# A hybrid decoder step in split fp16: first pairs by seven products at later blocks, spread forms of x, and range checks by ScalarE

## The chip, the cores and the metric

The kernel is one program on one core of a Trainium2 chip. Its time is the device time of one execution in microseconds (us). A core has TensorE (PE) for matrix products, VectorE (DVE), ScalarE (ACT) and GpSimd (POOL), and SyncE (SP), which here only issues transfers. PE's loads of stationary weights are listed apart as PEld; they run beside the matmuls. The DMA engines are shared by the queues of SP (q1), GpSimd (q0) and ScalarE (q10).

## The reference

One layer for 256 prompt tokens and 8 sample tokens, together T = 264 columns, with D_MODEL = 2048 and D_FF = 5504:

```python
h = h + 0.5 * swiglu(rmsnorm(h, norm_ffn1), ffn1_gate, ffn1_up, ffn1_down)
mix, C, n, m, buf = mixing_block(rmsnorm(h, norm_mix), w_in, ..., w_out, C_in, n_in, m_in, conv_in)
h = h + mix
h = h + 0.5 * swiglu(rmsnorm(h, norm_ffn2), ffn2_gate, ffn2_up, ffn2_down)
y = rmsnorm(h, norm_final)

def swiglu(x, wg, wu, wd):
    return (jax.nn.silu(x @ wg) * (x @ wu)) @ wd
```

The mixing block holds four mLSTM heads and a short gated convolution. All weights and inputs are float32. The change lies in the two SwiGLU stages, called the first and the second FFN here.

## The kernel before, in words

**Arithmetic.** Activations lie channels by tokens. Each float32 operand is scaled and split into an fp16 high part and an fp16 low part, and a product of 128 x 128 weights with 264 columns is three matmuls (`three`, L285 to L288): high weight by high x, high weight by low x, low weight by high x. `high` (L216) makes the high part on ScalarE, L219; `low` (L223) makes the low part on VectorE, L227. A weight tile is 128 x 8 x 128 in float32 (`wraw`), which becomes `whi` and `wlo`. `fetch` (L233) issues the load of the next tile of the plan on SP, and then its high and low parts. There are six buffers of each (`AHEAD` = 5, and one), and fetches run up to five tiles ahead of the products. With `lag` set, a tile's low part is issued one fetch later.

**Plan and start.** `weight_plan` (L82) lists the weight loads in order. The first four products of the first FFN (gate and up of blocks 0 and 1) run together in `products4` (L487), k by k, since x and the weights arrive k by k: `FIRST` (L45) lists the units as (first k, number of k, first product, number of products). A unit's weights are loaded and split while the one before is multiplied, and `ahead` (L854) loads h and cuts x from it.

**FFN.** D_FF is 43 blocks of 128, in two halves of 22 and 21 blocks (`HALVES`). A plain block is a gate product and an up product of 16 k each, one PSUM bank each (`product`, L290), followed by the scaling with the norm (L825, L831), Silu on ScalarE (L828) and the product of both (`activated`, L732). After each half come the products with the down weights.

**By seven products.** For the blocks of the list `SEVEN`, gate and up, the two halves of k and the two halves of the tokens are the 2 x 2 x 2 blocks of a product that needs seven multiplications instead of eight. Each is 8 k of three matmuls on 132 columns, L408, 168 matmuls in place of 96 on 264 columns. The stationary units are sums and differences of weight blocks. `prepare` (L316) sets down their making as steps: GpSimd's queue loads the weights (`load`, L326, L330, tile `sraw`, four loads of 512 KB for a block), `blocks` and `blocks_low` split three of them (tile `sa`), and `all_sums` and `sums_low` form four sums on VectorE (L354 to L356) and split them (tile `sb`). One step is taken per half of a plain product (`prepare_step`, L376), eight steps for a pair. The moving operands are four combinations of x for each of eight k: `Norm.form` (L652) scales h on ScalarE (`form_b`) and forms the differences on GpSimd (`form_t`, L662 to L664), and `form_split` (L667) splits them (tile `f`). The half products of block j run at blocks j and j + 2, with a plain block after each, so three blocks are a period: one pair and two plain blocks.

**Order.** The order on every engine is written out by hand. `tick` (L274) counts steps of the program, a whole one at the start of each product and half a one after its first eight k, and `at(delta, fn)` puts work at a later tick. In both FFNs the forms of x began at block 3, one each half or whole tick, and the steps of the first pair three blocks before the first entry of `SEVEN`, which was block 7 in both.

**The norm.** In the first FFN the squares of h are made in pairs (`square_pairs`, L683) on ScalarE and summed on VectorE; `finish` (L710) sums over channels by a matmul with ones (L622) and takes the inverse root. This happens after the products of block 2, and then blocks 0 to 2 are activated one after the other.

**Range checks.** `watch` (L530) sums, on VectorE (L536), the absolute values of the last 16 columns of every PSUM result into a column of `stat`; at the end these sums decide whether the scaled fp16 result is valid, or the whole step has to run again without the split. `twins` holds the same sums for the blocks by seven products.

Of the kernel before, what the change touches and what calls it, by code (L numbers as in the profile page):

```python
# [20 lines left out]
NFB = DFF // 128  # L21
# [23 lines left out]
FIRST = [(0, 1, 0, 2), (1, 1, 0, 2), (0, 1, 2, 2), (1, 1, 2, 2), (2, 1, 0, 4), (3, 1, 0, 4)]  # L45
# [4 lines left out]
SEVEN = list(range(7, 22, 3)) + list(range(22, NFB, 3))  # L50
# [31 lines left out]
def weight_plan(a, apart=()):  # L82
# [10 lines left out]
    def ffn(layer, first):  # L93
        gu, d = a[f"w{layer}gu"], a[f"w{layer}d"]
        for half, blocks in enumerate(HALVES):
            for j in blocks:
                if j >= first and j not in apart:
                    add((layer, "g", j), gu[j, 0], KB)
                    add((layer, "u", j), gu[j, 1], KB)
            for db in range(KB):  # L100
                b0, b1 = blocks[0], blocks[-1] + 1
                add((layer, "d", half, db), d[db][:, b0:b1, :], b1 - b0)
# [42 lines left out]
def step(ctx: ExitStack, tc: tile.TileContext, a: dict, shared, bad=None):  # L145
# [67 lines left out]
    plan = weight_plan(a, SEVEN if half_size else ())  # L213
# [102 lines left out]
    def prepare(pool, layer):  # L316
# [49 lines left out]
        for n, j in enumerate(SEVEN):  # L366
# [156 lines left out]
    if half_size:  # L523
# [3 lines left out]
        twins = const.tile([128, 2, 2 * len(SEVEN)], F32, name="twins")  # L527
        twin = iter(range(2 * len(SEVEN)))

    def watch(ps, rows=None):  # L530

        if half_size:
            j, n = len(stats), ps.shape[-1]
            stats.append(j)
            for r in rows or [slice(0, 128)]:
# [3 lines left out]
                )  # L539

# [177 lines left out]
    def ffn(layer, norm, done, start=None, end=None):  # L718
        with ExitStack() as stack:
# [4 lines left out]
            early = {}  # L724

# [50 lines left out]
            for half, blocks in enumerate(HALVES):  # L776
                act = {}
                step_end[0] = 8 * len(SEVEN) + 8

                order = []  # L780
                for i, j in enumerate(blocks):
                    if half_size and j in SEVEN:
                        order += [("seven", i, j, 0)]
                    elif half_size and j - 2 in SEVEN:
# [3 lines left out]
                for kind, i, j, c in order:  # L788
# [7 lines left out]
                    if first and start is not None:  # L796
# [4 lines left out]
                        for step, pairs in ((0, (0, 1, 2)), (1, (3, 4)), (1.5, (5, 6)), (2, (7,))):  # L801
                            at(step, norm.square_pairs, fpool, pairs)
# [3 lines left out]
                    if half_size and j == 3:  # L806
                        for k in range(8):
                            if k:
                                at((1.5, 2.5, 3, 4, 4.5, 5.5, 6)[k - 1], norm.form_split, k - 1)
                            at((1, 1.5, 2.5, 3, 4, 4.5, 5.5, 6)[k], norm.form, k)  # L810
                        at(6.5, norm.form_split, 7)
                        for fn, *what in steps.pop(-4):
                            fn(*what)
                    if half_size and j == SEVEN[0] - 3:
# [4 lines left out]
                    lag[0] = half_size and j >= 3  # L819
# [6 lines left out]
                    watch(pg)  # L826
# [6 lines left out]
                    watch(pu)  # L833
# [827 lines left out]
```

## Time and profile before

| | |
|---|---|
| median of three runs | 1831.66 us (1831.6 to 1832.43) |
| the profiled execution | 1831.9 us, its span 1830.2 us, mean granted clock 0.995 |
| PE busy | 1799.4 us, 17990 matmuls |
| DVE, ACT, POOL busy | 1400.8, 955.9, 248.2 us |
| high halves of weights (L219, `whi`) | 598 instructions, mean 997 ns |
| low halves of weights (L227, `wlo`) | 598 instructions, mean 1170 ns |
| read from memory | 366.72 MB, 207 GB/s over the span with what is written |

Busy time of PE overlaps from one matmul to the next, so a single matmul's duration (276 ns for 264 columns) is not its share of the time; the distance between starts is. A row of a wait names the engine and instruction that waited, the one that released it, the total, the count and the longest. In a timeline, a bracket holds the idle time ahead of the instruction and what ended it.

### The profile page before, as it was taken

What the parts mean: (1) busy time and instruction counts of PE and PEld (TensorE: products, weight loads), DVE (VectorE), ACT (ScalarE), POOL (GpSimd) and SP (SyncE); (2) the same over time, 40 slices, a digit from 0 to 9 for tenths busy, and PEclk for the clock granted to TensorE, in tenths of its full rate; (3) what the DMA queues carried; (4) which work ended last, traced back from release to release, by engine and by line L of the source; (5) the groups of instructions that cost most, each with busy time, mean ns of one, the idle gap of its engine ahead of it and who ended that gap; (6) DMA issues with size and microseconds to landing.
All of it is one profiled execution on the core that took longest, in us unless ns stands there. A gap on an engine that the chain in (4) does not pass through costs nothing. (4 is left out here: it accounts for less than half of the span.)

```text
span 1830.2 us, 42688 instructions
## 1 busy us (share of the span) xinstructions
PE 1799.4 (98%) x17990; PEld 1590.5 (87%) x17990; DVE 1400.8 (77%) x2151; ACT 955.9 (52%) x1332; POOL 248.2 (14%) x342
## 2 busy tenths in 40 slices
PE   7999999999999999999999999999999999999997
PEld 6789988899999888888888888889988889999886
DVE  6899985569998566888887866699986559998554
ACT  6655545345554445476666644565544335555442
POOL 1410000000000112222121022321000001000120
PEclk8999999999999999999999999999999999999999
DMA  9466567646564555888877656656567546654553
GB/s 313 151 212 216 188 199 240 204 151 216 183 222 135 197 194 183 273 279 301 274 268 256 221 190 222 205 194 211 202 196 246 192 153 208 205 202 160 179 194 100
DMA packets 118647, 381.34 MB, mean 208 GB/s; under 512 B 15116, under 2 KB 24940, under 8 KB 118448
## 3 DMA queue, kind: packets, MB, share of 16 engines
q1 hardware_dynamic: 95408, 300.19, 49.6%
q0 software_dynamic: 22080, 77.91, 12.4%
q8 instruction: 142, 2.33, 0.5%
q10 hardware_dynamic: 960, 0.45, 0.1%
q14 instruction: 57, 0.47, 0.1%
HBM read 366.72 MB, written 11.78 MB: 207 GB/s over the span
## 5 line engine op out<-in xcount | busy, mean ns | idle before, releaser
L227 DVE SCALAR_TENSOR_TENSOR wlo<-wraw,whi 128x1024 f16<-128x1024 f32 (+4 forms) x598 | 684.2, 1170 | 116.1 <-ACT whi L219 112.8
L219 ACT ACTIVATE whi<-wraw 128x1024 f16<-128x1024 f32 (+4 forms) x598 | 576.0, 997 | 165.1 <-PE ps L287 141.3
L288 PE MATMUL ps<-x,wlo 128*128 128x264 f16 x1920 | 530.0, 276 | 8.4 <-DVE wlo L227 8.4
L286 PE MATMUL ps<-x,whi 128*128 128x264 f16 x1920 | 529.9, 276 | 0.1
L287 PE MATMUL ps<-x,whi 128*128 128x264 f16 x1920 | 529.9, 276 | 0.0
L288 PEld LDWEIGHTS <-wlo 128*128 128x128 f16 x4490 | 439.3, 98 | 76.4 <-DVE wlo L227 12.0
L287 PEld LDWEIGHTS <-whi 128*128 128x128 f16 x4490 | 439.3, 98 | 65.7
L286 PEld LDWEIGHTS <-whi 128*128 128x128 f16 x4490 | 439.6, 98 | 64.9 <-issue 0.6
L288 PE MATMUL ps<-a,wlo 128*128 128x264 f16 (+2 forms) x1418 | 382.7, 273 | 0.4 <-DVE wlo L227 0.4
L286 PE MATMUL ps<-a,whi 128*128 128x264 f16 (+2 forms) x1418 | 382.8, 273 | 0.0
L287 PE MATMUL ps<-a,whi 128*128 128x264 f16 (+2 forms) x1418 | 382.8, 273 | 0.0
L286 PE MATMUL ps<-xm,whi 128*128 128x264 f16 x896 | 247.3, 276 | 0.0
L288 PE MATMUL ps<-xm,wlo 128*128 128x264 f16 x896 | 247.3, 276 | 0.0
L287 PE MATMUL ps<-xm,whi 128*128 128x264 f16 x896 | 247.3, 276 | 0.0
L219 ACT ACTIVATE sb<-ssum 128x2048 f16<-128x2048 f32 x48 | 91.7, 1911 | 185.2 <-DVE ssum L356 184.9
L408 PEld LDWEIGHTS <-sb 128*128 128x128 f16 x2304 | 134.4, 98 | 0.7
L841 DVE SCALAR_TENSOR_TENSOR h<-ps,h 128x264 f32<-128x264 f32 x62 | 26.7, 431 | 126.7 <-PE ps L288 126.7
L227 DVE SCALAR_TENSOR_TENSOR sb<-ssum,sb 128x2048 f16<-128x2048 f32 x48 | 110.3, 2298 | 7.5 <-ACT sb L219 4.9
L408 PE MATMUL ps<-f,sb 128*128 128x132 f16 x1728 | 103.3, 221 | 0.0
L408 PEld LDWEIGHTS <-sa 128*128 128x128 f16 x1728 | 101.3, 98 | 0.7
L330 POOL DMA_DIRECT2D sraw<-in_w1gu x48 | 34.6, 723 | 412.3 <-issue 406.0
L330 POOL DMA_DIRECT2D sraw<-in_w2gu x48 | 34.6, 723 | 412.3 <-issue 375.9
(255 smaller groups left out, 1682.6 us busy)
## 6 DMA issues: line engine op xcount, KB each, us to landing
wraw<-in_w2gu SPq DMA_DIRECT2D x124, 512.0 KB, 4.6
wraw<-in_w1gu SPq DMA_DIRECT2D x116, 512.0 KB, 4.7
wraw<-in_win SPq DMA_DIRECT2D x112, 512.0 KB, 5.9
wraw<-in_w1d SPq DMA_DIRECT2D x80, 448.0 KB, 4.0
wraw<-in_w2d SPq DMA_DIRECT2D x80, 448.0 KB, 4.0
sraw<-in_w1gu POOLq DMA_DIRECT2D x48, 512.0 KB, 5.4
sraw<-in_w2gu POOLq DMA_DIRECT2D x48, 512.0 KB, 5.1
wraw<-in_wout SPq DMA_DIRECT2D x32, 512.0 KB, 4.8
```

The costliest lines, as they stand in the source:

```text
L219: nc.scalar.activation(dst, src, AF.Copy, scale=scale)
L227: nc.vector.scalar_tensor_tensor(dst, src, scale, hi, op0=ALU.mult, op1=ALU.subtract)
L286: nc.tensor.matmul(ps, wh, xk[:, 0, :], start=first, stop=False)
L287: nc.tensor.matmul(ps, wh, xk[:, 1, :], start=False, stop=False)
L288: nc.tensor.matmul(ps, wl, xk[:, 0, :], start=False, stop=last)
L330: queue.dma_start(raw[:, 2 * g : 2 * g + 2], blocks[:, :, ks[c], :])
L408: nc.tensor.matmul(out, w[:, f, k, :], b(k)[:, part, :], start=(k + term == 0), stop=(k == 7 and term == 2),)
L841: nc.vector.scalar_tensor_tensor(h[db], ps, 0.5 / (sw * sa[layer]), h[db], op0=ALU.mult, op1=ALU.add)
```

## The change

Five edits in one diff:

- `FIRST`: at the start the units of the first two k hold all four products, one load of 256 KB each, instead of two units of two products.
- `SEVEN` becomes one list for each FFN. In the first FFN the list begins at block 10 instead of 7, so block 7 is a plain block and there are 11 pairs; the second keeps 7 and 12 pairs.
- The forms of x begin at block 3 in the first FFN and at block 1 in the second, and are spread evenly over the ticks up to the first pair, 1.5 and 1.25 ticks from one to the next. `lag` begins at the same blocks. The first pair's loads, so far issued in the program right after the forms are scheduled, come two ticks later.
- `square_pairs` takes two pairs at each of four ticks, instead of three, two, two and one.
- In the plain gate and up products, from the block on at which the steps of the first pair begin (7 in the first FFN, 4 in the second), the check is made by ScalarE: an activation Abs on 16 columns with a summed output. The up product of the last block of each half, the products before, and all others keep the check on VectorE.

```diff
-FIRST = [(0, 1, 0, 2), (1, 1, 0, 2), (0, 1, 2, 2), (1, 1, 2, 2), (2, 1, 0, 4), (3, 1, 0, 4)]
+FIRST = [(k, 1, 0, 4) for k in range(4)]
 FIRST += [(k, 2, j, 2) for k in range(4, KB, 2) for j in (0, 2)]
...
-SEVEN = list(range(7, 22, 3)) + list(range(22, NFB, 3))
+SEVEN = {n: list(range(j, 22, 3)) + list(range(22, NFB, 3)) for n, j in (("1", 10), ("2", 7))}
+PAIRS = sum(len(v) for v in SEVEN.values())
...
-        for n, j in enumerate(SEVEN):
+        for n, j in enumerate(SEVEN[layer]):
...
+    def watch_by_scalar(ps):
+
+        if half_size:
+            j, n = len(stats), ps.shape[-1]
+            stats.append(j)
+            nc.scalar.activation(
+                tmp.tile([128, SEEN], F32, tag="seen", name="seen", bufs=1),
+                ps[:, n - SEEN : n], AF.Abs, accum_out=stat[:, j : j + 1],
+            )
...
-                        for step, pairs in ((0, (0, 1, 2)), (1, (3, 4)), (1.5, (5, 6)), (2, (7,))):
+                        for step, pairs in ((0, (0, 1)), (1, (2, 3)), (1.5, (4, 5)), (2, (6, 7))):
                             at(step, norm.square_pairs, fpool, pairs)
...
-                    if half_size and j == 3:
-                        for k in range(8):
+                    if half_size and j == (3 if start is not None else 1):
+                        room = 2 * (sevens[0] - j) - 2
+                        for k in range(9):
+                            when = 1 + int(k * room / 8 * 2) / 2
                             if k:
-                                at((1.5, 2.5, 3, 4, 4.5, 5.5, 6)[k - 1], norm.form_split, k - 1)
-                            at((1, 1.5, 2.5, 3, 4, 4.5, 5.5, 6)[k], norm.form, k)
-                        at(6.5, norm.form_split, 7)
+                                at(when, norm.form_split, k - 1)
+                            if k < 8:
+                                at(when, norm.form, k)
+
                         for fn, *what in steps.pop(-4):
-                            fn(*what)
-                    if half_size and j == SEVEN[0] - 3:
+                            at(2, fn, *what)
+                    if half_size and j == sevens[0] - 3:
                         step_no[0] = -4
...
-                    lag[0] = half_size and j >= 3
+                    lag[0] = half_size and j >= (3 if start is not None else 1)
...
-                    watch(pg)
+                    (watch_by_scalar if step_no[0] is not None else watch)(pg)
...
-                    watch(pu)
+                    (watch_by_scalar if step_no[0] is not None and j < blocks[-1] else watch)(pu)
```

More of the change, by code (lines that the diff above doesn't have):

```diff
@@ L79, in mix_blocks, with weight_plan @@
     return {"h": head_blocks, "c": conv_blocks, "o": lambda ob: [O + ob]}[item[0]](n)
-def weight_plan(a, apart=()):
+def weight_plan(a, apart=None):
     plan = []
@@ L96, in ffn @@
             for j in blocks:
-                if j >= first and j not in apart:
+                if j >= first and (apart is None or j not in apart[layer]):
                     add((layer, "g", j), gu[j, 0], KB)
@@ L208, in step @@
         )
-    plan = weight_plan(a, SEVEN if half_size else ())
+    plan = weight_plan(a, SEVEN if half_size else None)
     ready = []
@@ L526, in step @@
         squares = const.tile([128, 6], F32, name="squares")
-        twins = const.tile([128, 2, 2 * len(SEVEN)], F32, name="twins")
-        twin = iter(range(2 * len(SEVEN)))
+        twins = const.tile([128, 2, PAIRS], F32, name="twins")
+        twin = iter(range(PAIRS))
     def watch(ps, rows=None):
@@ L724, in ffn @@
             early = {}
+            sevens = SEVEN[layer] if half_size else []
             def gate_up(j, which):
@@ L777, in ffn @@
                 act = {}
-                step_end[0] = 8 * len(SEVEN) + 8
+                step_end[0] = 8 * len(sevens) + 8
                 order = []
                 for i, j in enumerate(blocks):
-                    if half_size and j in SEVEN:
+                    if j in sevens:
                         order += [("seven", i, j, 0)]
-                    elif half_size and j - 2 in SEVEN:
+                    elif j - 2 in sevens:
                         order += [("seven", i - 2, j - 2, 1), ("one", i, j, 0)]
```

## The prediction

> **What bounds the kernel now.** I read the page first, then TensorE's list of waits over the whole span and over stretches of it, then the timeline of the start, the DMA queues in three stretches of the start, and the stretches where TensorE is not full.
>
> ```profile
> span 1830.2 us, 42688 instructions
> PE 1799.4 (98%) x17990; PEld 1590.5 (87%) x17990; DVE 1400.8 (77%) x2151; ACT 955.9 (52%) x1332; POOL 248.2 (14%) x342
> ```
>
> TensorE is without a matmul for only 1830.2 - 1799.4 = 30.8 us. A change that leaves the matmuls alone can win no more than a part of that. TensorE's own waits, first over the whole span (first line is the start's four products), then the second line's kind from 40 to 100, 100 to 200 and 1200 to 1300 us (wait, engine waited for, total, times, longest):
>
> ```profile
> PE ps L504 <- ACT whi L219: 9.0, 3, 6.7
> PE ps L288 <- DVE wlo L227: 8.8, 10, 2.3
> ...
> PE ps L288 <- DVE wlo L227: 5.9, 5, 2.3
> ...
> PE ps L288 <- DVE wlo L227: 1.1, 1, 1.1
> ...
> PE ps L288 <- DVE wlo L227: 1.4, 2, 1.1
> ```
>
> So there are two places: the start, and VectorE being late with the low halves of weights (wlo) around the first pair of either FFN. The start's timeline (start, duration, engine, idle time before and who ended it):
>
> ```profile
> 3.59 2.90 POOL L330 DMA_DIRECT2D sraw<-in_w1gu  x4
> ...
> 16.16 0.63 ACT L219 ACTIVATE whi<-wraw 128x512 f16<-128x512 f32 x1 [5.11 <-DMA wraw<-in_w1gu]
> ...
> 16.84 1.94 PE L504 MATMUL ps<-x,whi 128*128 128x264 f16 x8 [6.67 <-ACT whi L219]
> ...
> 38.70 1.06 ACT L219 ACTIVATE whi<-wraw 128x1024 f16<-128x1024 f32 x1 [0.23 <-DMA wraw<-in_w1gu]
> 39.66 2.76 ACT L687 ACTIVATE sq<-h 128x528 f32<-128x528 f32 x5
> ...
> 47.84 2.35 DVE L227 SCALAR_TENSOR_TENSOR wlo<-wraw,whi 128x1024 f16<-128x1024 f32 x2
> 50.11 0.42 DVE L604 SCALAR_TENSOR_TENSOR rs_q<-rs_y 128x264 f32<-128x264 f32 x1
> ```
>
> GpSimd issues four loads of 512 KB for the first pair at 3.59 us, although that pair is multiplied only near 100 us (a row further down). The next weights that the start needs arrive 5 us late. The queues (packets, MB, share of the 16 engines' time), 4 to 6 us, 6 to 14 us, 14 to 38 us; q1 is SP's, with the weights in use and x, and q0 is GpSimd's:
>
> ```profile
> q1 hardware_dynamic: 846, 0.46, 92.5%
> ...
> q0 software_dynamic: 541, 1.99, 68.4%
> q1 hardware_dynamic: 965, 0.57, 24.7%
> ...
> q1 hardware_dynamic: 5310, 8.03, 97.8%
> ```
>
> From 6 to 14 us the pair's loads hold two thirds of the engines' time. Then SP's queue is the bound until 38 us (97.8%): the fifth full weight tile lands at 38.70 us, the squares follow it on ScalarE at once, and from there squares, their sums, the norm's root and the first activations are one chain of ScalarE and VectorE. Stretches (length; PE, PEld, DVE, ACT, POOL busy; clock; DMA):
>
> ```profile
> 17.00:38.00 21.00, 21.00 (x171) 17.53 (x170) 17.80 (x30) 16.99 (x30) 0.00 (x0) 0.91 0.98 339
> 60.00:80.00 20.00, 18.89 (x167) 16.06 (x166) 17.51 (x24) 13.29 (x23) 12.51 (x14) 1.00 0.55 180
> 80.00:100.00 20.00, 15.14 (x134) 12.08 (x133) 18.71 (x20) 14.88 (x20) 11.51 (x11) 1.00 0.44 135
> 121.34:152.60 31.26, 31.26 (x362) 28.45 (x360) 28.69 (x40) 16.54 (x20) 2.88 (x4) 1.00 0.63 217
> 1200.00:1220.00 20.00, 18.55 (x199) 16.21 (x198) 19.11 (x22) 11.89 (x14) 6.53 (x7) 1.00 0.65 219
> ```
>
> From 60 to 100 us TensorE loses 1.11 + 4.86 = 5.97 us, while VectorE is nearly full. That is where the forms of x and the first pair's units fall together. The fourth row is one period of three blocks (a pair and two plain blocks) later: TensorE full, VectorE at 92%.
>
> **The change part by part.** The rows for the prices (line, engine, operation, shape, count | busy, mean ns | idle before); the last is a wait of the whole span:
>
> ```profile
> L227 DVE SCALAR_TENSOR_TENSOR wlo<-wraw,whi 128x1024 f16<-128x1024 f32 (+4 forms) x598 | 684.2, 1170 | 116.1 <-ACT whi L219 112.8 <-PE ps L504 2.6
> L227 DVE SCALAR_TENSOR_TENSOR sb<-ssum,sb 128x2048 f16<-128x2048 f32 x48 | 110.3, 2298 | 7.5 <-ACT sb L219 4.9
> L227 DVE SCALAR_TENSOR_TENSOR sa<-sraw,sa 128x1536 f16<-128x1536 f32 x48 | 84.7, 1765 | 3.3 <-ACT sa L219 0.2
> L356 DVE TENSOR_TENSOR ssum<-sraw,ssum 128x1024 f32<-128x1024 f32 x48 | 58.8, 1225 | 1.6
> L354 DVE TENSOR_TENSOR ssum<-sraw 128x512 f32<-128x512 f32 x48 | 33.3, 694 | 0.0
> L355 DVE TENSOR_TENSOR ssum<-ssum,sraw 128x512 f32<-128x512 f32 x48 | 33.2, 692 | 1.7
> L227 DVE SCALAR_TENSOR_TENSOR f<-form_t,f 128x528 f16<-128x528 f32 x16 | 13.1, 817 | 1.7 <-ACT f L219 1.5
> L825 DVE TENSOR_TENSOR ta<-ps,rstd 128x264 f32<-128x264 f32 x62 | 26.3, 424 | 10.8 <-PE ps L288 10.7
> L536 DVE TENSOR_REDUCE stat<-ps 128x1 f32<-128x16 f32 (+1 forms) x262 | 42.9, 164 | 0.0
> ...
> ACT f L219 <- POOL form_t L664: 18.6, 12, 2.1
> ```
>
> *Start.* The loads move from the head of GpSimd's queue to two ticks after block 3 begins, so behind the first form, which cannot run before block 3. SP's queue then keeps in 6 to 14 us the rate of 4 to 6 us, 0.46 / 2 = 0.23 MB/us. The 0.57 MB would take 2.5 us instead of 8, so everything behind it lands 5.5 us sooner. Does this reach the end? The fifth tile's landing starts the chain above, so the chain moves with it. TensorE could be earlier still (it makes up to 9.0 us of waits there), but then waits for the sum of the squares. I take -5.5. One bound is -7, if SP's queue ran at its later rate (8.03 / 24 = 0.33 MB/us, 1.7 us for the 0.57 MB) and the other is -3.5, if ScalarE and VectorE, at 17.0 and 17.8 of 21 us from 17 to 38, follow the earlier data 2 us late. The one unit per k of four blocks (256 KB instead of 128 KB) delays the first matmul by some half a microsecond, which the chain hides. If the chain were not there, that half would count. Two squares fewer ahead of the next unit and one more behind leave their sum where it is.
>
> *Forms and first pair of the first FFN.* VectorE needs for a plain block four wlo and four operations of 128x264: 4 x 1.17 + 4 x 0.424 = 6.4 us, plus 2 x 0.164 of checks. A pair's units cost 2 x (1.765 + 2.298 + 1.225 + 0.694 + 0.692) = 13.3 us, a form's low half 0.82. TensorE takes 10.8 us for a plain block (rows below), 32.4 for three. Before, blocks 4 to 6 hold three plain blocks, the first pair's units and six forms: 20.2 + 13.3 + 4.9 = 38.4 us, 6 too many, which is the loss that the rows from 60 to 100 us show. After, blocks 4 to 6 hold four forms and no units: 23.5 us, 8.9 to spare. Blocks 7 to 9 hold the units and three forms, without checks: 19.2 + 13.3 + 2.5 = 35.0, 2.6 too many, which the spare time of blocks 4 to 6 covers. A form now has 1.5 ticks instead of 0.5 or 1 until its split, so ScalarE's waits on GpSimd (last row) go too. Of the 5.9 + 1.1 us I keep 1.1, the wait at 60 us, since it comes from the activations of blocks 0 to 2, ahead of the forms, and 0.4 for blocks 7 to 9: -5.5. Bounds: -7.0, all of it, and -2.7, half of 5.5, if the in-order waits between ScalarE and VectorE keep the spare time from being used.
>
> *Second FFN.* The forms start at block 1 instead of 3, and the units at block 4 as before. Blocks 4 to 6 keep four of six forms and lose their checks there: 2 x 0.82 + 6 x 0.164 = 2.6 us less for VectorE, more than the 1.4 us of waits: -1.4, and 0 if that wait has another cause.
>
> *One pair fewer.* Block 7 of the first FFN becomes plain. On TensorE (three moments of the timeline):
>
> ```profile
> 98.25 0.28 PE L288 MATMUL ps<-x,wlo 128*128 128x264 f16 x1
> 99.37 1.83 PE L408 MATMUL ps<-x,sa 128*128 128x132 f16 x29
> ...
> 103.51 0.28 PE L286 MATMUL ps<-x,whi 128*128 128x264 f16 x1
> ```
>
> Ten matmuls of 264 columns take 1.12 us, 112 ns each, and the 72 of the half product between 99.37 and 103.51 take 57.5 ns each. A plain block has 96 of the first, 10.8 us, a pair 168 of the second, 9.7. The change costs +1.1, on the path, certain. (Two plain blocks and a pair make 31.3 us, as the fourth stretch shows.)
>
> *Checks by ScalarE.* The first FFN has 25 plain blocks from 7 on, the second 27 from 4 on: 104 products less the last of each half, 100 checks. VectorE loses 100 x 0.164 = 16 us. ScalarE gains an activation of 16 columns and the reading of its sum; nearest rows:
>
> ```profile
> L1281 ACT ACTIVATE den<-ps 128x1 f32<-128x1 f32 x8 | 1.4, 171 | 9.2 <-PE ps L1273 9.2
> L704 ACT ACTIVATE ta<-ps 128x136 f32<-128x136 f32 (+1 forms) x2 | 0.5, 274 | 0.0
> L1421 ACT ACTIVATION_READ_ACCUMULATOR jk<-jk 128x1 f32 x64 | 12.1, 189 | 0.0
> L828 ACT ACT_TABLE_LOAD x2 | 2.6, 1283 | 0.0
> ```
>
> Between 0.171 + 0.189 = 0.36 and 0.274 + 0.189 = 0.46 us; 16 columns are nearest the first, 0.37 us, 37 us in all. A period has four checks, 1.5 us more on ScalarE's 16.54 of 31.26. Behind a check wait the Silu, which waits for VectorE's product anyway, and after the second product the next high halves. TensorE is not waiting for anything in such a period, so neither the 16 us saved nor the 37 us added should be seen: 0, with bounds of +37 (all exposed) and -1. A gain would need a stall there, and outside the stretches above there are only 0.4 us.
>
> An Abs beside Silu might need another function table each time: the two loads at Silu's line are 1283 ns each, and no load stands at the Abs of L1281, though no run here has it beside Silu. On this the Trainium skill, "ScalarE: Activation LUTs", section "Table sets: the hidden batching unit", says that cheap functions, abs among them, are in every set. By that rule the sum has no such term. By the opposite, two loads at each of 100 checks would be 257 us of ScalarE.
>
> *The moved loads.* Their 2.1 MB now come near 55 us, when block 4's weights are wanted. In the stretch 60 to 80 DMA is at 0.55, so there is room: 0, at most +1.
>
> The sum: -5.5 - 5.5 - 1.4 + 1.1 = -11.3. The profiled execution took 1831.9 us (1.7 around its span), so 1820.6; the median of the three runs is 0.24 lower, 1831.66, which gives 1820.4.
>
> **The rivals.**
> 1. *The start's gain is lost on the way*: the chain behind the fifth tile is held by ScalarE and VectorE, not by DMA. For it: their 17.0 and 17.8 of 21 us. Against: ScalarE waits for DMA before that very tile (38.70). Then 1820.4 + 5.5 = 1826.
> 2. *The crowding moves to blocks 7 to 9 and keeps half*: for it the 35.0 against 32.4 us, against it the spare 8.9. 1820.4 + 2.7 = 1823.
> 3. *The moved loads starve blocks 4 and 5.* In 6 to 14 us SP's queue had 24.7% beside them. If it starved again for the whole transfer, 2.1 / 0.33 = 6.4 us would come back, 1826.8. Against: then SP's packets were short (0.57 MB in 965) and the loads' long (1.99 in 541); in block 4 both are long. The Trainium skill, "DMA: Bandwidth & Descriptors", section "Queues, rings and completion order", has each engine take turns between queues packet by packet. By that rule equal packets share evenly and the weights get 0.17 MB/us, close to what the period above moves, and the sum stays.
> 4. *Slower: ScalarE's checks are on the path.* Place: the second check of every plain block stands ahead of the next high half, whose low half VectorE makes at 92% load. If VectorE can't win back the delay, each check costs TensorE up to 0.37 us. From 11.3 / 37 = 31% exposed the change is slower than before; at half exposed it is 1820.4 + 18.5 = 1839. Against: VectorE gets 0.164 us back each time, and TensorE has no wait in the period.
> 5. *It doesn't do what it says*: a function table load at each check, 257 us on a ScalarE that is half free; 1840 and more.
>
> **How the numbers follow.** Forecast 0.70, rivals 1 to 5: 0.09, 0.08, 0.04, 0.05, 0.02; 0.02 for no difference at all. The time is the forecast's, 1820.4. The lower end takes the bounds of start, forms and second FFN, a little short of all three: 1831.7 - 6.5 - 6.5 - 1.4 + 1.1 = 1818.4, and 1.9 for what I can't price, to 1816.5. The upper end takes in rivals 1 to 3, to 1827. What this measurement can tell from no change is about 0.2%, 3.7 us. Faster holds the forecast and rivals 1 to 3, 0.91, less 0.02 for two of them together; slower is 4 and 5.
>
> **What would show it.** Right: no four loads ahead of 40 us and no wait of L504 above 2 us; the fifth full tile near 33 us; TensorE's waits on wlo from 40 to 200 us near 1.5 in place of 7.0, with about 1 of it at the end of block 3; none near 1200; 23 x 168 = 3864 narrow matmuls of L408 in place of 4032; ACT's Abs at about 0.2 us plus 0.19, no more table loads than before. Wrong: waits of TensorE on whi or wlo inside the later periods, table loads beside the checks, a wait for DMA near 55 us, or the first norm's column sums no earlier than before.

## The result and the profile after

The changed kernel takes 1816.88 us, median of six runs (1816.41 to 1817.96). The kernel before, run beside it, takes 1831.76 us (1831.0 to 1833.98). The ratio is 0.9917, with a 95% interval from 0.9905 to 0.993: faster by 14.9 us. The forecast was 1820.4, in the range 1816.5 to 1827. So the direction is right and the time lies at the lower edge of the range; 3.5 us of gain were not forecast.

The head of the page, after:

```profile
span 1815.3 us, 42573 instructions
...
PE 1799.1 (99%) x17918; PEld 1591.8 (88%) x17918; DVE 1379.5 (76%) x2041; ACT 968.7 (53%) x1529; POOL 237.1 (13%) x338
```

TensorE's list of waits over the span (wait, engine waited for, total, times, longest), after:

```profile
PE ps L633 <- DVE acc L705: 2.1, 1, 2.1
...
PE ps L505 <- ACT whi L220: 0.5, 1, 0.5
PE ps L289 <- DVE wlo L228: 0.4, 2, 0.2
```

Line numbers have moved by 1 to 15 (L288 is L289, L504 is L505, L622 is L633). TensorE has 72 matmuls fewer (168 less 96, one pair made plain) and is busy as long as before; its span is 14.9 us shorter. The wait for the start's weights went from 9.0 to 0.5, the waits for low halves from 8.8 to 0.4. A new wait of 2.1 us is at L633, the column sums of the first norm's squares.

The start's timeline, after:

```profile
31.31 1.06 ACT L220 ACTIVATE whi<-wraw 128x1024 f16<-128x1024 f32 x1 [1.45 <-DMA wraw<-in_w1gu]
32.27 2.23 ACT L698 ACTIVATE sq<-h 128x528 f32<-128x528 f32 x4
...
40.67 0.69 PE L633 MATMUL ps<-acc,ones 128*128 128x264 f32 x2 [2.10 <-DVE acc L705]
...
54.12 2.90 POOL L331 DMA_DIRECT2D sraw<-in_w1gu  x4
```

The pair's four loads are issued at 54.12 us instead of 3.59. The fifth full weight tile starts to be split at 31.31 instead of 38.70, and TensorE now arrives 2.1 us before the squares are summed. The queues (packets, MB, share of the 16 engines' time), after, 4 to 6, 6 to 14 and 14 to 31 us:

```profile
q1 hardware_dynamic: 779, 0.47, 78.7%
...
q1 hardware_dynamic: 3024, 2.85, 105.1%
...
q1 hardware_dynamic: 3124, 5.69, 99.9%
```

SP's queue carries 2.85 MB from 6 to 14 us, where it carried 0.57 before. TensorE's stretches (length; PE, PEld, DVE, ACT, POOL busy; clock; DMA share; GB/s), after:

```profile
60.00:80.00 20.00, 20.00 (x180) 17.41 (x178) 18.38 (x27) 15.02 (x23) 7.75 (x9) 1.00 0.97 349
80.00:100.00 20.00, 20.00 (x180) 17.39 (x179) 14.13 (x20) 13.42 (x24) 5.47 (x8) 1.00 0.63 204
100.00:120.00 20.00, 20.00 (x193) 17.58 (x192) 18.99 (x21) 11.46 (x17) 7.22 (x7) 1.00 0.57 188
```

From 60 to 120 us TensorE is full; before, it lost 5.97 us of the first 40. To see where the time went I compare single matmuls that stand at the same place of the work: the end of block 3's wait (before) or the same matmul (after), the first down product of the first FFN, the first product of the second FFN and its first down product. Before, and then after:

```profile
61.31 0.29 PE L288 MATMUL ps<-x,wlo 128*128 128x264 f16 x1 [1.11 <-DVE wlo L227]
...
256.96 0.28 PE L286 MATMUL ps<-a,whi 128*128 128x264 f16 x1
...
1130.51 0.28 PE L286 MATMUL ps<-x,whi 128*128 128x264 f16 x1
...
1364.64 0.28 PE L286 MATMUL ps<-a,whi 128*128 128x264 f16 x1
```

```profile
53.91 0.29 PE L289 MATMUL ps<-x,wlo 128*128 128x264 f16 x1
...
243.53 0.28 PE L287 MATMUL ps<-a,whi 128*128 128x264 f16 x1
...
1117.08 0.28 PE L287 MATMUL ps<-x,whi 128*128 128x264 f16 x1
...
1349.42 0.28 PE L287 MATMUL ps<-a,whi 128*128 128x264 f16 x1
```

The differences are -7.40, -13.43, -13.43 and -15.22. So the start gives -7.40, the first half of the first FFN another -6.03, nothing changes up to the second FFN, and its first half gives -1.79. The last matmul still starts 15.22 us sooner (1805.60 instead of 1820.82); the span is 14.9 us shorter, so 0.3 us are lost behind the matmuls, and their cause stays open.

### The profile page after: what moved, and what is told of

Its sections match the earlier page's. It is cut to its first block, busy times and chain, and to the rows that moved or that the text cites. A ratio compares the mean times of both kernels' runs of the same rounds, so it can differ in the third digit from the quotient of the medians.

```text
span 1815.3 us, 42573 instructions
## 1 busy us (share of the span) xinstructions
PE 1799.1 (99%) x17918; PEld 1591.8 (88%) x17918; DVE 1379.5 (76%) x2041; ACT 968.7 (53%) x1529; POOL 237.1 (13%) x338
## 5 line engine op out<-in xcount | busy, mean ns | idle before, releaser
L228 DVE SCALAR_TENSOR_TENSOR wlo<-wraw,whi 128x1024 f16<-128x1024 f32 (+2 forms) x600 | 688.0, 1171 | 110.4 <-ACT whi L220 109.6
L220 ACT ACTIVATE whi<-wraw 128x1024 f16<-128x1024 f32 (+2 forms) x600 | 580.2, 1001 | 159.9 <-PE ps L288 139.2
L287 PE MATMUL ps<-x,whi 128*128 128x264 f16 x1952 | 539.6, 276 | 0.0
L289 PE MATMUL ps<-x,wlo 128*128 128x264 f16 x1952 | 539.5, 276 | 0.0
L288 PE MATMUL ps<-x,whi 128*128 128x264 f16 x1952 | 539.5, 276 | 0.0
L288 PEld LDWEIGHTS <-whi 128*128 128x128 f16 x4522 | 442.7, 98 | 66.5
L289 PEld LDWEIGHTS <-wlo 128*128 128x128 f16 x4522 | 442.7, 98 | 66.4 <-DVE wlo L228 1.0
L289 PE MATMUL ps<-a,wlo 128*128 128x264 f16 (+2 forms) x1418 | 382.7, 273 | 0.4 <-DVE wlo L228 0.4
L288 PE MATMUL ps<-a,whi 128*128 128x264 f16 (+2 forms) x1418 | 382.8, 273 | 0.0
L289 PE MATMUL ps<-xm,wlo 128*128 128x264 f16 x896 | 247.3, 276 | 0.0
L288 PE MATMUL ps<-xm,whi 128*128 128x264 f16 x896 | 247.3, 276 | 0.0
L409 PEld LDWEIGHTS <-sb 128*128 128x128 f16 x2208 | 128.8, 98 | 0.7
L228 DVE SCALAR_TENSOR_TENSOR sb<-ssum,sb 128x2048 f16<-128x2048 f32 x46 | 105.2, 2288 | 8.7 <-ACT sb L220 8.7
L409 PE MATMUL ps<-f,sb 128*128 128x132 f16 x1656 | 99.0, 221 | 0.0
L409 PEld LDWEIGHTS <-sa 128*128 128x128 f16 x1656 | 97.1, 98 | 0.7
L228 DVE SCALAR_TENSOR_TENSOR sa<-sraw,sa 128x1536 f16<-128x1536 f32 x46 | 81.2, 1766 | 3.1
```

What stands on the lines that cost most here:

```text
L220: nc.scalar.activation(dst, src, AF.Copy, scale=scale)
L228: nc.vector.scalar_tensor_tensor(dst, src, scale, hi, op0=ALU.mult, op1=ALU.subtract)
L287: nc.tensor.matmul(ps, wh, xk[:, 0, :], start=first, stop=False)
L288: nc.tensor.matmul(ps, wh, xk[:, 1, :], start=False, stop=False)
L289: nc.tensor.matmul(ps, wl, xk[:, 0, :], start=False, stop=last)
L409: nc.tensor.matmul(out, w[:, f, k, :], b(k)[:, part, :], start=(k + term == 0), stop=(k == 7 and term == 2),)
```

## Experiments

Each kernel is the kernel before or the changed one with one or two edits. Ratios are to the kernel before, run on the same chip beside it. Its median was 1832.34 us beside `b_loads`, `a_loads`, `a_forms` and `a_vec`, 1832.54 beside `a_pair7`, `a_first`, `a_dear` and `a_pool`, and 1833.19 beside `b_act`, `c_early`, `c_form` and `c_best`. Comparisons with the changed kernel go by ratios, its own being 0.9917 [0.9905, 0.993].

### The moved loads alone, and all but them

`b_loads` is the kernel before with only the first pair's loads moved:

```diff
                         for fn, *what in steps.pop(-4):
-                            fn(*what)
+                            at(2, fn, *what)
```

> The kernel before with one edit: the first pair's loads two ticks after block 3 begins. Theory 1 (the loads' 2.1 MB at the head of the DMA engines delay the whole chain of the start): the fifth full weight tile arrives near 32 us instead of 38.7, and the time falls by 6 to 7.5 us, to about 1825; TensorE's 7 us of waits on low halves from 40 to 200 us stay as they are. Rival (ScalarE and VectorE hold the chain at the start, or the first units must be single ones of four products for the gain): less than 3 us.

`a_loads` is the changed kernel with the opposite edit, the loads back at the head of GpSimd's queue:

```diff
                         for fn, *what in steps.pop(-4):
-                            at(2, fn, *what)
+                            fn(*what)
```

> The changed kernel with the loads back at the head of GpSimd's queue, all else as changed. Theory 1: it loses 6 to 7.5 us, to about 1824, with a wait of 4 us or more of TensorE inside the four products again. Rival: with units of four products and six buffers the start stands the loads, loss under 2 us.

Measured: `b_loads` 1826.89 us, ratio 0.9972 [0.9961, 0.9983]; `a_loads` 1822.87 us, ratio 0.9949 [0.9934, 0.9964]. The queues of `a_loads` from 6 to 14 us:

```profile
q0 software_dynamic: 539, 1.99, 66.8%
q1 hardware_dynamic: 1223, 0.85, 36.1%
```

and TensorE's wait for the start's weights in `a_loads`:

```profile
PE ps L505 <- ACT whi L220: 6.9, 2, 6.4
```

In `b_loads` the fifth full tile starts at 31.32 us, as in the changed kernel; in `a_loads` at 36.65. So the loads at the head of the queue are what delayed the start, and moving them is worth 0.28% by itself (5.1 us) and 0.32% (5.9 us) inside the change, both a little less than the 6 to 7.5 us expected. The rest of the change without it makes 0.51%.

That 0.28 and 0.51 come near the whole 0.83 is in part luck. The matmul behind block 3's wait, at 61.31 us before and 53.91 after, stands at 59.26 in `a_loads` and in `b_loads` at

```profile
53.93 0.29 PE L288 MATMUL ps<-x,wlo 128*128 128x264 f16 x1 [1.10 <-DVE wlo L227]
```

So in these traces the moved loads alone bring the whole 7.4 us of the start. With the loads still at the head, the other edits of the start (`FIRST` and the squares) bring about 2 us, in this one trace, which are not there any more once the loads are moved. `b_loads` in turn loses about 2 us again later.

Where it loses them is seen in two places: it is 7.38 us ahead of the kernel before at the end of block 3, 6.11 at the first down product (250.84 us), and 5.27 at the second FFN's (1359.37 us). TensorE's waits for low halves from 45 to 110 us and from 1100 to 1350 us:

```profile
PE ps L288 <- DVE wlo L227: 6.7, 6, 2.3
...
PE ps L288 <- DVE wlo L227: 2.3, 2, 1.2
```

The first is nearly as before (5.9 + 1.1), but behind the wait of 2.3 us, which the kernel before has too, 15 matmuls from 90.86 us on start 220 ns apart instead of 112, which costs 1.6 us (see the last section). The second was 1.4: the same line of code also moves the loads of the second FFN's first pair, and with the old crowded forms that alone costs 0.9 us there. By the trace the gain of the start is therefore 7.4 us, and not the 5.1 that the 0.28% shows.

### The forms' ticks and the later pair

`a_forms` is the changed kernel with the old ticks of the forms, from block 3 in both FFNs; the first pair of the first FFN stays at block 10.

```diff
-                    if half_size and j == (3 if start is not None else 1):
-                        room = 2 * (sevens[0] - j) - 2
-                        for k in range(9):
-                            when = 1 + int(k * room / 8 * 2) / 2
+                    if half_size and j == 3:
+                        for k in range(8):
...
+                                at((1.5, 2.5, 3, 4, 4.5, 5.5, 6)[k - 1], norm.form_split, k - 1)
+                            at((1, 1.5, 2.5, 3, 4, 4.5, 5.5, 6)[k], norm.form, k)
+                        at(6.5, norm.form_split, 7)
...
-                    lag[0] = half_size and j >= (3 if start is not None else 1)
+                    lag[0] = half_size and j >= 3
```

> The changed kernel with the forms of x from block 3 in both FFNs at the old ticks, the first pair at block 10 as changed. Theory 2a (what cost 6 us was that forms and the first pair's units fell on the same blocks; the later pair alone mends that in the first FFN): the first FFN keeps its gain, since blocks 4 and 5 take the forms without units (20.2 + 6 x 0.82 = 25 us of VectorE in 32), and only the second FFN loses its 1.8 us: about 1818.5. Theory 2b (the spacing is what counts, since ScalarE waits for GpSimd's forms in order): 3 to 6 us come back in the first FFN too, 1821 to 1824.

`a_pair7` is the changed kernel with the first pair of the first FFN back at block 7; the forms then spread over three blocks.

```diff
-... for n, j in (("1", 10), ("2", 7))}
+... for n, j in (("1", 7), ("2", 7))}
```

> The changed kernel with the first FFN's list from block 7 again (12 pairs in both FFNs); the forms keep their even spacing, which is then 0.75 ticks. Theory 2 (forms and units on the same blocks cost what VectorE has too much): blocks 4 to 6 need 20.2 - 1.0 + 13.3 + some 4.9 = 37.4 us of VectorE in 32.4 of TensorE, so 4 to 5 us of waits come back less the 1.1 us that a pair saves, about 1820. Rival (the even spacing and the checks by ScalarE were enough, and the later pair only costs): 1.1 us faster than the changed kernel, 1815.8.

Measured: `a_forms` 1822.51 us, ratio 0.9945 [0.993, 0.996]; `a_pair7` 1823.49 us, ratio 0.9952 [0.9937, 0.9968]. Waits for low halves in `a_forms`, 45 to 110 us and 1100 to 1350 us:

```profile
PE ps L289 <- DVE wlo L228: 3.5, 5, 1.1
...
PE ps L289 <- DVE wlo L228: 2.3, 2, 1.3
```

in `a_pair7`, 45 to 110 us:

```profile
PE ps L289 <- DVE wlo L228: 6.9, 6, 2.3
```

and the stretch of `a_pair7` in which most of it falls:

```profile
80.00:100.00 20.00, 16.08 (x159) 13.50 (x160) 19.83 (x21) 12.41 (x19) 10.28 (x10) 0.91 0.50 173
```

With the pair at 7, all of the loss stays: VectorE is busy for 19.83 of 20 us and TensorE for 16.08. That is 0.35%, 6.4 us, although this kernel has the cheaper extra pair (1.1 us). I had expected about 1820, because I took the loss by crowding at 4 to 5 us; by the waits it is 6.9, of which 1.1 is that at the end of block 3. Between that point and the first down product this kernel takes 197.08 us and the changed one 189.63; with the pair's 1.1 the crowding costs 8.6 us. The five other waits, 5.8 us, make 6.9 of it with the part that the list leaves out (below), and the rest goes with slow matmuls behind the longest wait (last section). So the later pair is what frees the first FFN.

But `a_forms` shows that it is not all: with VectorE's load moved out of blocks 4 to 6, the old ticks, half a tick or one apart, still make four waits behind that of block 3 (2.4 of the 3.5 us). The stretch up to the first down product takes 192.68 us instead of 189.63, so 3 of the 6 us come back, as theory 2b of the expectation had it. Over both FFNs it is 0.28%. The spare time of VectorE alone did not remove the waits; the spacing is needed too.

In the second FFN `a_forms` has waits of 2.3 us where the changed kernel has none. There it takes back four things together, the block at which the forms begin, their ticks, `lag`, and with the block the moment of the pair's loads; which of them counts is not shown.

`c_form` then sets the forms of the first FFN half a tick later still, away from the activations of blocks 0 to 2.

```diff
-                            when = 1 + int(k * room / 8 * 2) / 2
+                            when = (1.5 if start is not None else 1) + int(k * room / 8 * 2) / 2
```

> The changed kernel with the first FFN's forms half a tick later, so that block 4's first weights are split ahead of the first form. They come 1.1 us earlier (0.9 of form_b on ScalarE, 0.26 of VectorE beside GpSimd). Theory 1b: TensorE reaches block 4 at that same time (no gap at 53.9 us now), so alone this gains 0 to 0.3 us. Rival (the split of block 4's first weights alone sets that time): 1.1 us gained.

Measured: 1817.24 us, ratio 0.9918 [0.9905, 0.9932], the changed kernel's. No wait is left there that it could take away: what the changed kernel waits for is the sum of the squares, earlier. It has a wait of its own instead, at the first pair (about 124 us), for the low half of a form:

```profile
PE ps L409 <- DVE f L228: 0.7, 1, 0.7
```

### The range checks

`a_vec` is the changed kernel with all checks on VectorE, `b_act` the kernel before with only the checks on ScalarE (from block 4 on in both FFNs), `a_dear` the changed kernel with each of ScalarE's checks made three times.

```diff
-                    (watch_by_scalar if step_no[0] is not None else watch)(pg)
+                    watch(pg)
...
-                    (watch_by_scalar if step_no[0] is not None and j < blocks[-1] else watch)(pu)
+                    watch(pu)
```

> The changed kernel with all checks on VectorE. Theory 3 (the checks lie beside other work on either engine): the same within 1 us; TensorE's smallest lead of weights over use in blocks 7 to 9 falls from 4.3 us to about 3. Rival (VectorE at 92% needs the 16 us): 1 to 5 us slower, with waits on low halves in the first pair's blocks.

```diff
-                    watch(pg)
+                    (watch_by_scalar if step_no[0] is not None else watch)(pg)
...
-                    watch(pu)
+                    (watch_by_scalar if step_no[0] is not None and j < blocks[-1] else watch)(pu)
```

> The kernel before with one edit: the checks of plain gate and up products by ScalarE from block 4 on in both FFNs. Theory 3 (beside other work on either engine): within 1 us of the kernel before, but for the crowded blocks 4 to 6, where VectorE gets 6 x 0.164 = 1.0 us back, so 0 to 1 us faster. Rival 4: 100 checks of 0.364 us at the share that the tripled checks showed (13.6% of 73 us) would be 5 us slower.

```diff
-            nc.scalar.activation(
-                ...
-            )
+            for _ in range(3):
+                nc.scalar.activation(
+                    ...
+                )
```

> The changed kernel with each of ScalarE's 100 checks made three times over, which adds 200 x 0.364 = 73 us to ScalarE's work and nothing else. Theory 3 (the checks lie beside other work, with some 5 us of lead at the least): within 1 us of the changed kernel. Rival 4 of the prediction (checks ahead of the high halves are on the path): with a third exposed 24 us slower, with a tenth 7 us.

Measured: `a_vec` 1817.08 us, ratio 0.9912 [0.9896, 0.9927]; `b_act` 1832.93 us, ratio 0.9999 [0.999, 1.0008]; `a_dear` 1826.76 us, ratio 0.9968 [0.9956, 0.998]. The checks by ScalarE bring nothing and cost nothing: not beside the other edits, not alone. Their price and the function table loads of Silu's line in the changed kernel:

```profile
L547 ACT ACTIVATION_READ_ACCUMULATOR seen<-ps 128x1 f32 x100 | 19.3, 193 | 0.0
L547 ACT ACTIVATE seen<-ps 128x16 f32<-128x16 f32 x100 | 17.1, 171 | 84.8 <-DVE ta L840 84.8
...
L843 ACT ACT_TABLE_LOAD x2 | 2.6, 1283 | 0.0
```

100 checks at 171 + 193 ns, 36.4 us, without a table load of their own: there are still two at Silu's line. On this the rule of the Trainium skill that the prediction named ("ScalarE: Activation LUTs", "Table sets: the hidden batching unit") agrees with the trace. One period of three blocks, first with the checks on VectorE (`a_vec`) and then the changed kernel:

```profile
138.00:169.30 31.30, 31.30 (x364) 28.49 (x362) 26.85 (x34) 15.26 (x18) 2.88 (x4) 1.00 0.55 183
```

```profile
138.00:169.30 31.30, 31.30 (x365) 28.49 (x363) 27.57 (x33) 16.68 (x24) 2.89 (x4) 1.00 0.58 191
```

TensorE is full in both, and ScalarE has half of its time free. `a_dear` shows how much more there is room for. It was expected to move the time by a microsecond at most and moved it by 0.51%, 9.3 us of 75.7 us added (two rows below: 58.1 + 54.0 less 36.4). The price in `a_dear`:

```profile
L548 ACT ACTIVATION_READ_ACCUMULATOR seen<-ps 128x1 f32 x300 | 58.1, 194 | 0.1
L548 ACT ACTIVATE seen<-ps 128x16 f32<-128x16 f32 x300 | 54.0, 180 | 75.3 <-DVE ta L841 69.0
```

and TensorE's waits in `a_dear` over the whole span that the changed kernel has not, or hardly:

```profile
PE ps L409 <- DVE sb L228: 3.5, 4, 1.1
PE ps L289 <- DVE wlo L228: 2.8, 4, 1.1
PE ps L287 <- ACT whi L220: 2.8, 3, 1.5
```

The waits are not in the plain periods, but where ScalarE has most to do: at the first down products (around 268 and 1380 us), and at the last pairs of each second half, whose sums (`sb`) come late. Two of these waits are followed by 15 and 14 matmuls that start 220 ns apart (from 269.09 and 1381.94 us), another 3.1 us in the profiled execution. So a single check is hidden everywhere, and three are hidden in the periods but not at these edges. My expectation went by the free time of a period alone, and that was the mistake.

### The start's units and squares

`a_first` is the changed kernel with the old `FIRST` and the old order of the squares:

```diff
-FIRST = [(k, 1, 0, 4) for k in range(4)]
+FIRST = [(0, 1, 0, 2), (1, 1, 0, 2), (0, 1, 2, 2), (1, 1, 2, 2), (2, 1, 0, 4), (3, 1, 0, 4)]
...
-                        for step, pairs in ((0, (0, 1)), (1, (2, 3)), (1.5, (4, 5)), (2, (6, 7))):
+                        for step, pairs in ((0, (0, 1, 2)), (1, (3, 4)), (1.5, (5, 6)), (2, (7,))):
```

> The changed kernel with the old units of the start (six, the first four of two products) and the old order of the squares. Theory 1 (once the loads are gone, the fifth full tile's arrival sets the start, and the units' order doesn't change the bytes): the same within 1 us, the fifth tile again near 31.3. Rival (the larger units bring part of the 7.4 us): 1.5 us or more slower.

Measured: 1816.56 us, ratio 0.9913 [0.99, 0.9927], the changed kernel's. From 6 to 14 us SP's queue carries

```profile
q1 hardware_dynamic: 2676, 2.44, 96.5%
```

where the changed kernel carries 2.85 MB. The larger loads do fill the queue better, by 0.4 MB, but the end does not see it. The fifth full tile is at 31.82 us against 31.31; among five other kernels here whose start is the changed kernel's, that moment lies between 30.61 and 32.46, so half a microsecond can't be told apart.

What holds the start now? By the trace it is the chain behind the fifth tile, with TensorE waiting 2.1 us for it. Two kernels shorten this chain. `a_pool` has GpSimd make the squares of each k as h arrives, instead of ScalarE later:

```diff
-                        for step, pairs in ((0, (0, 1)), (1, (2, 3)), (1.5, (4, 5)), (2, (6, 7))):
-                            at(step, norm.square_pairs, fpool, pairs)
+                        if not half_size:
+                            for step, pairs in ((0, (0, 1)), (1, (2, 3)), (1.5, (4, 5)), (2, (6, 7))):
+                                at(step, norm.square_pairs, fpool, pairs)
...
                 n1.cut(kb)
+                if half_size:
+                    n1.square(kb)
```

> The changed kernel with the squares of h for the first norm and their sum made by GpSimd block by block as h arrives, instead of by ScalarE and VectorE after the fifth weight tile. GpSimd needs 16 x (0.63 + 0.90) = 24 us, so the sum is there near 30 us instead of 40.5. Theory 1b (what is left of the start is the chain fifth tile, squares, root, activations): the wait of 2.1 us on the sum goes and with it the slow clock behind it (1.5 us), block 4 starts 2 to 4 us earlier, about 1813 to 1815. Rival (GpSimd beside VectorE slows the low halves from 1.22 to 1.48 us, and the weights' chain holds the start): no gain, or 1 us lost.

`c_early` has ScalarE square the first eight k during the units of k = 8 to 14, and the others at the first two ticks:

```diff
-                        for step, pairs in ((0, (0, 1)), (1, (2, 3)), (1.5, (4, 5)), (2, (6, 7))):
+                        for step, pairs in ((0, (4, 5)), (1, (6, 7))) if half_size else ((0, range(8)),):
                             at(step, norm.square_pairs, fpool, pairs)
...
+            if half_size and k0 >= 8:
+                n1.square_pairs(n1.fpool, ((k0 - 8) // 2,))
```

> The changed kernel with the first four of eight squares (and their sums) made while the four products run, at the units of k = 8 to 14, and the others right after. Theory 1b (what is left of the start is the serial work of VectorE between the fifth tile and the root, 7 sums of 0.70 us, and TensorE waits 2.1 us for it and then runs 1.5 us longer at half clock): the wait on the sum goes, block 4's first low half is made 2 to 2.8 us earlier, about 1814.5. Rival (the work only moves into the four products, where VectorE has 2.36 of 2.7 us, and delays them): under 0.5 us gained.

`c_best` has this edit and that of `c_form`.

> Both of these edits. Theory 1b: with the wait gone TensorE could reach block 4 near 50.3 us instead of 53.9, and the weights are there near 50: 3 to 3.6 us gained, more than the two alone together, about 1813.5. Rival: no more than the better of the two.

Measured: `a_pool` 1822.13 us, ratio 0.9944 [0.993, 0.9958]: 0.27% or 5 us lost, where the rival expectation had 1 us at most. `c_early` 1815.68 us, ratio 0.9911 [0.9898, 0.9925]. `c_best` 1814.14 us, ratio 0.9899 [0.9884, 0.9914]. TensorE's new waits in `a_pool`:

```profile
PE ps L505 <- DVE wlo L228: 4.7, 8, 0.7
PE ps L505 <- DVE x L228: 1.2, 6, 0.4
```

VectorE's two groups of the start and GpSimd's squares in `a_pool`, 4 to 38 us:

```profile
L228 DVE SCALAR_TENSOR_TENSOR wlo<-wraw,whi 128x512 f16<-128x512 f32 x16 | 17.5, 1124 | 0.3 <-ACT whi L220 0.3
L688 POOL TENSOR_TENSOR sq<-h 128x264 f32<-128x264 f32 x15 | 14.1, 938 | 1.4 <-DMA h<-in_xt 1.4
L228 DVE SCALAR_TENSOR_TENSOR x<-h,gains,x 128x264 f16<-128x264 f32 x16 | 13.2, 851 | 0.8 <-ACT x L220 0.8
```

The same two groups in the changed kernel:

```profile
L228 DVE SCALAR_TENSOR_TENSOR wlo<-wraw,whi 128x512 f16<-128x512 f32 x16 | 11.0, 691 | 2.4 <-ACT whi L220 2.0
L228 DVE SCALAR_TENSOR_TENSOR x<-h,gains,x 128x264 f16<-128x264 f32 x16 | 7.3, 488 | 0.9 <-ACT x L220 0.8
```

The same 32 instructions of VectorE take 30.7 us instead of 18.3 while GpSimd makes the squares and their sum. VectorE becomes the bound of the start.

`c_early` shows the chain undisturbed: the wait for the sum is gone, and TensorE's only wait from 28 to 60 us this one, in the timeline:

```profile
50.54 0.29 PE L289 MATMUL ps<-x,wlo 128*128 128x264 f16 x1 [0.73 <-DVE wlo L228]
```

That is the wait at the end of block 3 from before, which the changed kernel had lost to the wait for the sum. As a single edit the gain is not clear of the measurement. `c_best` is: its slowest run, 1815.79, is below the fastest of `c_form` on the same chip, 1816.33, and the medians are 3.1 us apart. Since these two differ in the squares alone, the earlier squares are worth that beside the later forms. Against the changed kernel both edits together bring 0.18% or 3.3 us, as expected (3 to 3.6). It has the lowest median here, 18.5 us under the kernel before by its ratio, but its runs overlap those of `c_early` (1814.52 to 1817.32), and like `c_form` it waits 0.7 us for a form at the first pair. That the later forms add to the earlier squares is therefore not shown.

## Why the prediction was right, and where its sizes were off

**Start.** Right in place and mechanism; the term was mis-sized, -5.5 for a measured -7.40, beyond its bound of -7. `b_loads`, with the loads alone, has -7.38. The step that failed is the rate: "SP's queue then keeps in 6 to 14 us the rate of 4 to 6 us", 0.23 MB/us. That is the rate of the first microseconds only. Measured is 2.85 MB in 8 us, 0.356 MB/us, and 5.69 MB in 17 us, 0.335, after it. With 2.28 MB more by 14 us and 0.335 MB/us behind it, everything lands 6.8 us sooner. Short packets alone don't explain the low rate: from 6 to 8 us the changed kernel carries 0.67 MB in 1084 packets, hardly longer than the 0.46 MB in 846, at 0.335 MB/us already. Why the first ones are slower stays open. The bound of -7 named the later rate, 0.33, but the prediction's own working gives 8 - 1.7 = 6.3 us at that rate and not 7; that 6.3 should have been the value taken. The remaining half microsecond is within what the moment of the fifth tile differs between kernels with the same start. That it reaches the end was argued from ScalarE's wait for DMA ahead of that tile, and holds. The matmul of the column sums stood in the timeline of before, without a wait, at

```profile
48.54 0.61 PE L622 MATMUL ps<-acc,ones 128*128 128x264 f32 x2
```

and stands at 40.67 now, 7.9 us sooner.

**The 1.1 us kept for the wait at 60 us.** It was kept because its cause, the activations of blocks 0 to 2, was not touched. In the changed kernel that wait is not there, and the reason is not a cheaper activation: TensorE itself comes late to this place, by 2.1 us of waiting for the sum and a stretch at a lower clock. `c_early` removes that wait, and 0.7 of the old one is back. The prediction had seen that TensorE "then waits for the sum of the squares", and did not carry this on to the next wait.

**Forms and first pair of the first FFN.** Right in mechanism, mis-sized: from block 4 to the down products -6.03, where the prediction's terms give -5.5 + 1.1 = -4.4. Two parts of the term failed. The 0.4 kept for blocks 7 to 9 did not come, since no wait is left there. And the loss before was larger than taken. The waits were added up as listed, but each costs more than the list says: it begins at the end of the last matmul, 276 ns after its start, while matmuls without a wait start 112 ns apart, so each stall costs another 0.16 us. Behind the wait at 61.31 the listed waits of before are 5.9 + 1.1 - 1.1 = 5.9 us in five stalls, and two more matmuls, too little for the list, start 0.14 and 0.27 us late; 5.9 + 5 x 0.16 + 0.4 = 7.1, and with the plain block's 1.1 that is -6.0, against -6.03 measured. VectorE's surplus of 6 us was low too: its 1.17 for a wlo is a mean over five shapes, and the shape of these blocks, 128x1024, takes 1.229, which makes the surplus 6.7. The bound of -2.7, in which "the in-order waits between ScalarE and VectorE keep the spare time from being used", is seen in part in `a_forms`: without the spacing, 3 us come back.

**Second FFN.** -1.79 for a predicted -1.4: the two listed waits and 2 x 0.16 = 1.7. The checks, which the prediction counted there, have no part in it: between the same two matmuls `b_act` takes 234.15 us and the kernel before 234.14. The moved loads alone make the waits 2.3 (`b_loads`), and the edits that `a_forms` takes back remove all of it.

**One pair fewer.** 72 matmuls fewer, 168 x 23 = 3864 narrow ones (552 + 1104 + 1656 + 552 by their four groups of L409). Its +1.1 has no experiment of its own; the sum above closes with it.

**Checks.** 0, as predicted, at 0.364 us a check (predicted 0.37). `a_vec` and `b_act` agree. Rival 4 (checks on the path) falls for one check; `a_dear` shows that its mechanism exists, at 12% exposure (9.3 of 75.7), away from the place that I had named.

**Moved loads.** 0, as predicted. From 60 to 80 us the DMA share is 0.97 instead of 0.55 and TensorE is full; rival 3, weights that starve, did not come. Beside SP's short packets the loads had 66.8 to 68.4% of the engines' time; beside its long ones TensorE waits for nothing. From 10 to 13 us before, when both queues had work, the loads sent 267 packets with 0.98 MB and SP's queue 290 with 0.18; from 59 to 66 us after, with packets of like length:

```profile
q0 software_dynamic: 357, 1.31, 52.7%
q1 hardware_dynamic: 336, 1.25, 47.6%
```

The weights got 1.25 MB in 7 us there, 0.18 MB/us, for the 0.17 of the prediction. In both stretches the two queues sent nearly as many packets. The rule of the Trainium skill named there ("DMA: Bandwidth & Descriptors", "Queues, rings and completion order") is in keeping with both, though no run changes the packets alone.

**FIRST and squares.** 0, as predicted, once the loads are moved (`a_first`). With the loads at the head of the queue they bring about 2 us by the trace of `a_loads`, which the prediction did not see.

**The rivals.** 1 (start's gain lost) falls by `b_loads`; 2 (crowding moves to blocks 7 to 9) by the full stretches after; 5 (table loads) by the two loads at Silu's line. All mis-sized terms erred on one side, -1.9, -1.6 and -0.4, less the 0.3 at the end: -3.6, the distance from the forecast. Had each stall been counted with its 0.16 and the queue with its later rate, the sum would have been near 1818. The measured time is also below 1818.4, the sum that took the bounds of the start, the forms and the second FFN. What held it in the range is the 1.9 us "for what I can't price", which no row stands behind; that they were enough is luck.

## What to carry to other kernels

Look for loads that are issued long before their use at the head of a second queue: they take the engines' time from the loads that the start waits for, and moving them behind the start was the largest single gain here. When a stage has one crowded stretch, it takes both to empty it, work moved out of it and the rest spaced so that engines that work in the written order can use the room; and when a wait is removed, follow the chain to the next thing that is late, and count each removed stall by the distance of starts, not by the listed idle time. Offloading a few tenths of a microsecond from a busy engine that nothing waits for brings nothing.

## What was not expected of the hardware

- *VectorE beside GpSimd.* In `a_pool` a low half of 128x512 takes 1124 ns instead of 691 and one of 128x264 takes 851 instead of 488, while GpSimd squares and adds 128x264 tiles in float32. The Trainium skill, "GPSIMD Engine Reference", section "8. Key points", names contention of the two where a VectorE instruction has two inputs in SBUF, as these have; here that costs a factor of 1.6 to 1.7, and a job "for an idle engine" made the kernel 0.27% slower than the changed one.
- *The clock after a short wait.* After the 2.1 us wait in the changed kernel TensorE runs at a lower clock for some microseconds. Its matmuls in the timeline:

```profile
41.38 0.43 PE L288 MATMUL ps<-x,whi 128*128 128x264 f16 x1
41.59 0.43 PE L289 MATMUL ps<-x,wlo 128*128 128x264 f16 x1
```

  and two stretches of the changed kernel:

```profile
38.00:42.00 4.00, 1.90 (x12) 1.23 (x10) 3.76 (x6) 3.34 (x5) 0.00 (x0) 0.90 0.41 142
42.00:46.00 4.00, 4.00 (x26) 3.00 (x24) 3.30 (x9) 2.03 (x3) 0.00 (x0) 0.67 0.74 239
```

  Starts are some 220 ns apart instead of 112, from 41.38 to 44.66 us. These 15 take 3.3 us where they would take 1.7, so the wait costs about 1.6 us more than its length. The Trainium skill, "TensorE: Matmul & The Clock Gate", section "Part 1: The HAM clock gate (the "warmup" mystery)", puts the drop after about 3.4 us without work. Here it followed a shorter pause, and the measurement decides. In `b_loads` the slow matmuls come 0.5 us after a wait of 2.3 us, in `a_pair7` 1.4 us after one as long (a stretch of 20 us there is at 0.91). It isn't always so: before, a wait of 2.3 us between 80 and 100 us left the clock at 1.00, and `a_dear` has one of 2.4 us at the sum of the squares without slow matmuls behind it. What decides between the two is not shown.
- *The start's scatter.* The moment of the fifth tile differs by up to 1.9 us between traces of kernels with the same start (30.61 to 32.46 us). A single trace's start says nothing about half a microsecond.
